# Splitting the first transfers and widening a normalisation in a two-layer hybrid attention kernel

## The chip, the cores and the metric

The kernel runs on one core of one Trainium2 chip. A core has five engines that run side by side, each with its own queue of instructions: TensorE (PE; its weight loads are listed as PEld), VectorE (DVE), ScalarE (ACT), GpSimd (POOL) and SyncE (SP), which here issues all the transfers (DMA) between the chip's main memory and the on-chip memory. The metric is the device time of one execution in microseconds (us); less is better.

## The reference

Two layers, each on 256 positions of 1024 values:

```python
h = x @ w_in                      # split into gm_u, gm_v, gm_z, nq, nkc, ... , mq, mz
y_gm  = gmlp_mixer(gm_u, gm_v, gm_z, ...)      # gated MLP over chunks of 128 positions
y_nsa = nsa_mixer(...)            # compressed, selected and windowed attention, gated
y_mem = memory_mixer(mq, mz, mem, w_mem_kv)    # attention over 256 memory rows
y = concatenate([y_gm, y_nsa, y_mem]) @ w_out
x = layer_norm(ALPHA * x + y, ln_g, ln_b)

# gmlp_mixer
u = gelu(u); v = gelu(v).reshape(B, S, 4, 64)
v = layer_norm(v, ln_g, ln_b)     # mean and variance over the 64 values of each group
s = einsum('gij,bnjgc->bnigc', ws * causal, v) + bs
return u * s * silu(z)
```

## The kernel before, in words

Values are float32. For a product, each operand is split into a high part, which ScalarE casts to the type that TensorE reads (a CAST in the trace), and a low part, which VectorE subtracts (`split`); a product is three matmuls, high by high, high by low and low by high (`mm3`). So every weight chunk of 128 x 512 values costs one transfer of 256 KB, one cast and one subtraction, and then its matmuls. A weight matrix is eight such chunks (`weights`, `eighth`), one for each 128 of the 1024 input values. Tile `w` holds the split chunk, and the raw chunk lies in `wr` or, where that is idle, in another tile (`gz`, `mz`, `gu`, `gv`, `kmr`, `vmr`, `qr`, `nz`), so a transfer into `gz` at the start is the first weight chunk and one into `mz` the second.

At the start `load_T` brings the transposed x in five pieces: two of 128 KB (x pieces 0 and 1, for input values 0 to 127 and 128 to 255) and three of 256 KB (two pieces' worth each). Their raw tile is called `dup`. The weights of tile B (keys) come in between, chunk by chunk. `proj` multiplies 128 positions of x with the chunks of a weight matrix, chunk by chunk into one accumulator of 128 x 512, and `keys` uses it for both halves of the positions with B. Before the first data arrive, nine multiplications of a zeroed tile (`warm`, tile `pr`) are in TensorE's queue.

In `gmlp` the normalisation goes over eight units, two position blocks times four groups, of 128 x 64 values in tile `gv`. Mean and variance come from two small instructions per unit (`gst`, `gmv`), the reciprocal root from one VectorE instruction and a power on GpSimd (`veps`, `grs`), then each unit is normalised by one instruction with two scalars per row, and all are multiplied with the weights and added to the bias in `glt` (tile `qr`) by two wide instructions. TensorE then multiplies with the causal matrix, and VectorE applies bias and gate (`gv<-tp,pt,gu`).

The order of all instructions is not the order of the code. Each call is recorded by the class `Plan`, with its cost from a formula (`cost`, lines 138 to 164) and its dependences (`record`). `schedule` searches 1000 times, with random changes to priorities, for the order with the least modelled length (`pack` places instructions by list scheduling, each engine in order), and `emit` issues that order. A number in `nc.rank` overrides the priority: the first x pieces have rank 2 times their index, B's chunk k has 2k + 1, and a lower rank goes first. At most eight transfers are in flight. As the search records everything through one line, all instructions in the profile carry the line number 336, and the tile names tell them apart.

Of the kernel before, what the change touches and what calls it, by code (L numbers as in the profile page):

```python
# [14 lines left out]
ALU = mybir.AluOpType  # L15
# [3 lines left out]
P = 128  # L19
S = 256  # L20
NB = S // P
# [3 lines left out]
HD = 64  # L25
# [10 lines left out]
SB, SN, S0, ZP = (2,), (0, 1), (0, 1, 2), ()  # L36
ORDER = "FWDMNERGPQ01", "WDFMNERGP0Q1"
WARM, WN = 9, 512
XV, BFIRST = (), 0
WIDE = (20, 20)  # L40
PHASE = (3, 0)

# [48 lines left out]
class Plan:  # L91
# [45 lines left out]
    @staticmethod  # L137
    def cost(engine, op, out, ins, kw):
        n = int(np.prod(out.shape[1:]))
        if engine == "tensor":  # L140
            if op == "transpose":
                return 110.0
            if ins[0].dtype == F32:
                return 2 * (55 + 0.42 * n)
            return max(0.4453 * n + 4, 108.0 if ins[0].dtype == F32R else 30.0)
        if "dma" in op:
            return 500.0
        src = max([int(np.prod(a.shape[1:])) for a in ins] + [1])
        in_psum = any(a.tensor._space == PSUM for a in ins)
        if engine == "scalar":  # L150
            extra = sum(isinstance(kw.get(k), bass.AP) for k in ("bias", "accum_out")) + (op == "mul" and len(ins) > 1)
            return (52 if in_psum else 97) + n / 1.2 + 93 * extra
        if engine == "gpsimd":
            if op == "tensor_scalar":
                return (60 if n < 8 else 240) + 0.87 * n
            if op == "tensor_tensor" and n <= 8:
                return 300 + 165 * n
            return 160 + 2.1 * n
        if op == "reciprocal":
            return 60 + 8.3 * n  # L160
        one = 62 * sum(int(np.prod(a.shape[1:])) == 1 for a in ins)
        if not in_psum and op in ("tensor_copy", "tensor_scalar", "tensor_scalar_add"):
            return 65 + 0.52 * n + one
        return 70 + 1.04 * max(src, n) + one
# [14 lines left out]
    def record(self, eng, op, args, kw):  # L179
        aps = [a for a in list(args) + list(kw.values()) if isinstance(a, bass.AP)]  # L180
        out = [args[0]] + ([kw["accum_out"]] if "accum_out" in kw else [])
        dma = "dma" in op
        o = {"i": len(self.ops), "eng": eng, "op": op, "args": args, "kw": kw, "pre": set(), "dma": dma, "rank": self.rank,
             "table": {AF.Exp: "exp", AF.Tanh: "exp", AF.Gelu: "gelu"}.get(args[2]) if op == "activation" else None,
             "cost": self.cost(eng.name, op, args[0], aps[1:], kw),
             "port": not dma and self.shares(eng.name, op, args[0], aps[1:])}
        if dma:
            o["bytes"] = int(np.prod(args[0].shape)) * 4
            o["issue"] = self.DMA_ISSUE[hasattr(args[1].tensor, "subtile_deps")]
        for ap in aps:  # L190
            name = ap.tensor.name
            if not hasattr(ap.tensor, "subtile_deps"):
                continue
            w = any(ap is x for x in out)
            p0, p1, mask = self.region(ap)
            psum = ap.tensor._space == PSUM
            keep = []
            for e in self.live.setdefault(name, []):
                q0, q1, m, ew, j = e
                if psum:  # L200
                    hit = w or ew or self.ops[j]["eng"] is not eng
                else:
                    hit = (w or ew) and p0 < q1 and q0 < p1 and mask & m
                if j != o["i"] and hit:
                    o["pre"].add(j)
                    if w and p0 <= q0 and q1 <= p1 and (mask & m) == m:
                        continue
                keep.append(e)
            keep.append((p0, p1, mask, w, o["i"]))
            self.live[name] = keep  # L210
        if self.after is not None:
            o["pre"].add(self.after)
        self.ops.append(o)
# [126 lines left out]
def hymba_kernel(ctx: ExitStack, tc: tile.TileContext, xT, xN, memT, w512, wC, cw1, par, gln, lngb, const, out):  # L340
# [30 lines left out]
    def split(h, l, src, eng=None):  # L371
        nc.scalar.copy(h, src)
        (eng or nc.vector).tensor_sub(l, src, h)


    def load_T(src, hl, tag, urgent=False):

        for half in range(2):
            raw = buf(tag, [P, 4, S])
            for k0, k1 in ([(0, 1), (1, 2), (2, 4)], [(0, 2), (2, 4)])[half]:  # L380
                ks = slice(4 * half + k0, 4 * half + k1)
                nc.rank = 2 * ks.start if urgent else None
                nc.sync.dma_start(raw[:, k0:k1], src[:, ks])
                h, l = [t[:, ks] for t in hl]
                if urgent and ks.start in XV:
                    nc.vector.tensor_copy(h, raw[:, k0:k1])
                    nc.vector.tensor_sub(l, raw[:, k0:k1], h)
                else:
                    split(h, l, raw[:, k0:k1])
        nc.rank = None  # L390

    def eighth(name, l, k):

        t = buf("w", [P, 2 * NCC], F32R)
        if name == "W1":
            t = t[:, :8 * P].rearrange("p (j h n) -> p h j n", j=4, h=2)
            src = cw1[l, k].rearrange("p (j n) -> p j n", j=4)
        else:
            n = NCC if name == "C" else 512
            t = t[:, :2 * n].rearrange("p (h n) -> p h n", h=2)  # L400
            src = wC[l, k] if name == "C" else (w512[int(name[1]), W512.index("M"), k] if name[0] == "M" else w512[l, W512.index(name), k])
        early = (name, l) == ("B", 0)
        nc.rank = 2 * k + (1 if k or not BFIRST else -1) if early else None
        raws.append(None)
        tags = IDLE.get((name, l), [])
        i = len(raws) % (len(tags) + 4)
        raw = buf(EARLY[k] if early else tags[i] if i < len(tags) else "wr", [P] + list(src.shape)[1:])
        nc.sync.dma_start(raw, src)
        split(t[:, 0], t[:, 1], raw)
        nc.rank = None  # L410
        return t

# [3 lines left out]
    def mm3(acc, a, b, first, last, **kw):  # L416
# [2 lines left out]
        nc.tensor.matmul(acc, ah, bl, start=False, stop=False, **kw)  # L419
        nc.tensor.matmul(acc, al, bh, start=False, stop=last, **kw)  # L420

    def proj(tT, w, b, c0, n, acc):
        ts = slice(b * P, (b + 1) * P)
        for k in range(KC):
            mm3(acc, [x[:, k, ts] for x in tT], [w[k][:, j, c0:c0 + n] for j in range(2)], k == 0, k == KC - 1)
        return acc

    def projT2(tT, w, c0):
# [119 lines left out]
    for l in range(L):  # L548
# [33 lines left out]
            stack_q(qs[:, :, :, b * P:(b + 1) * P], tp.rearrange("p (x n) -> p x n", x=4), SCALE)  # L582

        wb, wa = weights("B", l), weights("A", l)
        for b in range(NB):
            keys(b, proj(x_T, wb, b, 0, 512, bank("acc")))
            queries(b, proj(x_T, wa, b, 0, 512, bank("acc")))
# [27 lines left out]
        def gmlp(gu, gv, glt):  # L615
            st = buf("gst", [P, NB * G, 6], F32)
            mv = buf("gmv", [P, NB * G, 2], F32)
            units = [(i, gv[:, i // G, i % G * HD:(i % G + 1) * HD]) for i in range(NB * G)]
            for i, v in units:
                nc.vector.bn_stats(st[:, i, :], v)  # L620
                nc.vector.bn_aggr(mv[:, i, :], st[:, i, :])
            rs = buf("grs", [P, NB * G], F32)
            rstd_of(rs, mv[:, :, 1])
            for i, v in units:
                nc.vector.tensor_scalar(v, v, mv[:, i, 0:1], rs[:, i:i + 1], ALU.subtract, ALU.mult)
            nc.vector.tensor_mul(gv, gv, glt[:, 0:1, :].to_broadcast([P, NB, 256]))
            nc.vector.tensor_add(gv, gv, glt[:, 1:2, :].to_broadcast([P, NB, 256]))
            nc.gpsimd.tensor_mul(gu, gu, gz)
            gs = bank("tp").rearrange("p (g b d) -> p g b d", g=G, b=NB)
            for g in range(G):  # L630
                nc.tensor.matmul(gs[:, g], wsT[:, g, :], gv[:, :, g * HD:(g + 1) * HD], start=True, stop=True)
            for g in range(G):
                c = slice(g * HD, (g + 1) * HD)
                nc.vector.scalar_tensor_tensor(gv[:, :, c], gs[:, g], bsT[:, g:g + 1], gu[:, :, c], ALU.add, ALU.mult)
            tp = bank("tp")
            for c in range(2):
                for b in range(NB):
                    nc.tensor.transpose(tp[:, (NB * c + b) * P:(NB * c + b + 1) * P], gv[:, b, c * P:(c + 1) * P], ident)
            t3 = tp.rearrange("p (c t) -> p c t", c=2)
            h, lo = [t[:, :2, :] for t in y_T]  # L640
            nc.scalar.mul(h, t3, 0.5)
            nc.vector.scalar_tensor_tensor(lo, t3, 0.5, h, ALU.mult, ALU.subtract)
# [380 lines left out]
```

## Time and profile before

| | |
|---|---|
| median of 3 runs | 295.34 us (295.31 to 295.97) |
| the profiled execution | 295.48 us |
| its span, first to last instruction | 293.7 us |
| instructions | 5787 |

The profile is of one execution. Its times are counted from the first instruction, and the rest of the execution's time lies around the span. Busy time is the time in which an engine had an instruction under way; the ends of matmuls are modelled. In a row of the timeline stand the start, the time to the end of the row's last instruction, the engine, the operation, the tile written and the tiles read, shapes, the number of instructions, and in brackets how long the engine was idle before and what it waited for. The 40 slices of the page show TensorE at 8 or 9 tenths until the last three.

### The profile page before, as it was taken

The page shows a single profiled execution, that of the slowest core. Times are in us where ns is not written, and L with a number is a line of the kernel's source. Part 1 is how long each engine was busy: PE and PEld are TensorE (multiplying, and loading weights), DVE is VectorE, ACT ScalarE, POOL GpSimd, SP SyncE. Part 2 cuts the span into 40 slices and gives each one's busy share as a digit, 9 for nine tenths or more (in the row PEclk, how much of TensorE's full clock was granted, in tenths as well). Part 3 has the DMA queues.
Part 4 walks back from the last instruction along what each step waited for, and adds up shares of the span by engine and source line. Part 5 has one row for each costly group of instructions (what it writes and reads, how often), then busy time and mean ns, then how long its engine had stood idle before and what let it go on. Part 6 is the DMA issues. An engine that isn't in the chain of part 4 may idle for free.

```text
span 293.7 us, 5787 instructions
## 1 busy us (share of the span) xinstructions
PE 281.6 (96%) x1837; PEld 248.1 (84%) x1837; DVE 266.2 (91%) x662; ACT 224.9 (77%) x537; POOL 64.2 (22%) x89
## 2 busy tenths in 40 slices
PE   8999999999999999999999999999999999899990
PEld 3688899988999899777778888898998899687890
DVE  3889889789979998999999998899899999999985
ACT  4877786888998877999776177689969979989400
POOL 0003029304220435020010100491201146000011
PEclk9999999999999999999999999999999999999996
DMA  6999897597766715677257739847685433300012
GB/s 190 388 389 388 251 264 225 141 265 222 236 159 182 233 39 158 209 232 208 72 161 211 225 97 259 271 136 252 190 233 172 121 134 105 111 36 0 2 71 73
DMA packets 30062, 53.66 MB, mean 183 GB/s; under 512 B 3536, under 2 KB 6352, under 8 KB 29904
## 3 DMA queue, kind: packets, MB, share of 16 engines
q1 hardware_dynamic: 30032, 53.30, 58.6%
q8 instruction: 14, 0.23, 0.3%
q14 instruction: 16, 0.13, 0.2%
HBM read 49.09 MB, written 1.05 MB: 171 GB/s over the span
## 4 chain that ended last, share of the span: by engine, by line
PE 63%; ACT 15%; DVE 12%; DMA 5%; issue 3%; SPq 0%; DVEq 0%; ACTq 0%
PE o L336 31%; PE acc L336 22%; PE tp L336 6%; ACT w L336 5%; PE sc L336 3%; ACT pr L336 3%; DVE w L336 2%; DMA wr<-in_w_dram 2%; DMA dup<-dup 2%; DMA mz<-in_w_dram 1%; ACT dup L336 1%; DVE gv L336 1%; DVE pr L336 1%; ACT pTh L336 1%; ACT csTr L336 1%
## 5 line engine op out<-in xcount | busy, mean ns | idle before, releaser
L336 DVE TENSOR_TENSOR w<-wr,w 128x512 fp32r<-128x512 f32 (+1 forms) x84 | 58.9, 715 | 4.8 <-ACT w L336 4.7
L336 PE MATMUL acc<-w,xTh 128*128 128x512 f32 (+2 forms) x208 | 58.3, 349 | 0.0
L336 ACT CAST w<-wr 128x512 fp32r<-128x512 f32 (+1 forms) x84 | 50.6, 624 | 6.3 <-DMA wr<-in_w_dram 2.2
L336 PE MATMUL o<-xTh,w 128*128 128x256 f32 x224 | 44.6, 284 | 0.1
L336 PE MATMUL acc<-w,yTh 128*128 128x256 f32 (+1 forms) x160 | 44.2, 344 | 0.4 <-ACT yTh L336 0.4
L336 POOL TENSOR_SCALAR pr<-pr,fs 128x256 f32<-128x256 f32 (+1 forms) x36 | 23.9, 674 | 92.6 <-DVE fs L336 52.1
L336 PEld LDWEIGHTS acc<-w,xTh 128*128 128x128 f32 x208 | 36.8, 189 | 5.2 <-ACT w L336 0.3
L336 PEld LDWEIGHTS o<-xTh,w 128*128 128x128 f32 x224 | 35.7, 189 | 0.8 <-DVE yt L336 0.3
L336 PE MATMUL acc<-w,xTl 128*128 128x512 f32 (+2 forms) x104 | 35.7, 349 | 0.0
L336 ACT ACTIVATE pr<-pr,nm 128x128 f32<-128x128 f32 (+1 forms) x64 | 28.7, 451 | 9.0 <-DVE nm L336 8.9
L336 PE MATMUL o<-w,xTh 128*128 128x512 f32 (+2 forms) x112 | 35.1, 374 | 0.4 <-DVE w L336 0.2
L336 PE MATMUL o<-xTl,w 128*128 128x256 f32 x112 | 31.3, 283 | 0.0
L336 PEld LDWEIGHTS acc<-w,yTh 128*128 128x128 f32 x160 | 27.2, 188 | 4.3 <-ACT yTh L336 1.1
L336 POOL TENSOR_TENSOR dup<-pr,pt 64x120 f32<-64x120 f32 x32 | 21.8, 692 | 37.2 <-ACT pr L336 30.6
L336 PE MATMUL acc<-w,yTl 128*128 128x512 f32 (+1 forms) x80 | 27.1, 347 | 0.1
L336 PEld LDWEIGHTS o<-w,xTh 128*128 128x128 f32 x112 | 20.1, 189 | 5.2 <-DVE w L336 1.2
L336 DVE TENSOR_TENSOR pTl<-tp,pTh 128x512 fp32r<-128x512 f32 x32 | 21.4, 678 | 0.6 <-ACT pTh L336 0.4
L336 PE MATMUL tp<-ct,pr 128*128 128x128 f32 x128 | 21.7, 275 | 0.2 <-DVE pr L336 0.2
L336 PEld LDWEIGHTS acc<-w,xTl 128*128 128x128 f32 x104 | 19.5, 188 | 2.3
L336 PEld LDWEIGHTS o<-xTl,w 128*128 128x128 f32 x112 | 20.9, 188 | 0.3
L336 ACT CAST pTh<-tp 128x512 fp32r<-128x512 f32 x32 | 18.4, 586 | 3.0 <-PE tp L336 1.7
L336 PE MATMUL o<-w,xTl 128*128 128x512 f32 (+2 forms) x56 | 20.5, 366 | 0.0
(202 smaller groups left out, 705.2 us busy)
## 6 DMA issues: line engine op xcount, KB each, us to landing
wr<-in_w_dram SPq DMA_DIRECT2D x69, 256.0 KB, 3.4
gz<-in_w_dram SPq DMA_DIRECT2D x14, 256.0 KB, 2.9
mz<-in_w_dram SPq DMA_DIRECT2D x14, 256.0 KB, 3.6
gu<-in_w_dram SPq DMA_DIRECT2D x8, 256.0 KB, 4.0
wr<-in_cw_dram SPq DMA_DIRECT2D x8, 256.0 KB, 3.6
dup<-in_lngb_dram SPq DMA_DIRECT2D x4, 512.0 KB, 5.3
wr<-in_wC_dram SPq DMA_DIRECT2D x7, 268.0 KB, 5.7
gv<-in_w_dram SPq DMA_DIRECT2D x7, 256.0 KB, 3.5
```

Of the source, the lines that this page charges most:

```text
L336: getattr(o["eng"].engine, o["op"])(*o["args"], **o["kw"])
```

## The change

There are three edits. First, x piece 0 comes as two transfers of 128 positions each, and B's first weight chunk as two transfers of 256 columns each, each half with its own cast and subtraction; in `proj` the matmuls of the first chunk of B in layer 0 are done by column halves. Second, in `gmlp` the eight narrow normalising instructions become two wide ones with broadcast operands (subtract the mean, multiply with the reciprocal root), and the weights are multiplied in between. Third, some prices of the search change: ScalarE instructions on fewer than 128 rows cost 60 ns more, GpSimd's general price rises by 40 ns and by 40 more for fewer rows, and the masked maximum (`tensor_tensor_reduce`) loses 62 ns.

```diff
@@ Plan.cost
-            return (52 if in_psum else 97) + n / 1.2 + 93 * extra
+            return (52 if in_psum else 97) + n / 1.2 + 93 * extra + (60 if out.shape[0] < P else 0)
...
-            return 160 + 2.1 * n
+            return 200 + 2.1 * n + (40 if out.shape[0] < P else 0)
...
-        one = 62 * sum(int(np.prod(a.shape[1:])) == 1 for a in ins)
+        one = 62 * sum(int(np.prod(a.shape[1:])) == 1 for a in ins) if op != "tensor_tensor_reduce" else 0
@@ Plan.record
-                    hit = w or ew or self.ops[j]["eng"] is not eng
+                    hit = j != o["i"] and (w or ew or self.ops[j]["eng"] is not eng)
@@ load_T
-                nc.sync.dma_start(raw[:, k0:k1], src[:, ks])
-                h, l = [t[:, ks] for t in hl]
-                if urgent and ks.start in XV:
...
-                    split(h, l, raw[:, k0:k1])
+                for ts in [slice(0, P), slice(P, S)] if urgent and not ks.start else [slice(0, S)]:
+                    nc.sync.dma_start(raw[:, k0:k1, ts], src[:, ks, ts])
+                    split(*[t[:, ks, ts] for t in hl], raw[:, k0:k1, ts])
+                    nc.rank = nc.rank if nc.rank is None else nc.rank + 1.5
@@ eighth
-        nc.sync.dma_start(raw, src)
-        split(t[:, 0], t[:, 1], raw)
+        n = src.shape[-1]
+        for cs in [slice(0, n // 2), slice(n // 2, n)] if early and not k else [slice(0, n)]:
+            nc.sync.dma_start(raw[..., cs], src[..., cs])
+            split(t[:, 0, ..., cs], t[:, 1, ..., cs], raw[..., cs])
@@ proj   (first = wb in layer 0, else None)
-            mm3(acc, [x[:, k, ts] for x in tT], [w[k][:, j, c0:c0 + n] for j in range(2)], k == 0, k == KC - 1)
+            cut = n // 2 if w is first and not k else n
+            for c in range(0, n, cut):
+                mm3(acc[:, c:c + cut], [x[:, k, ts] for x in tT], [w[k][:, j, c0 + c:c0 + c + cut] for j in range(2)],
+                    k == 0 and c == 0, k == KC - 1, **({"skip_group_check": True} if w is first else {}))
@@ gmlp
-            for i, v in units:
-                nc.vector.tensor_scalar(v, v, mv[:, i, 0:1], rs[:, i:i + 1], ALU.subtract, ALU.mult)
+            g3 = gv.rearrange("p b (g d) -> p (b g) d", g=G)
+            nc.vector.tensor_sub(g3, g3, mv[:, :, 0].unsqueeze(2).to_broadcast([P, NB * G, HD]))
             nc.vector.tensor_mul(gv, gv, glt[:, 0:1, :].to_broadcast([P, NB, 256]))
+            nc.vector.tensor_mul(g3, g3, rs.unsqueeze(2).to_broadcast([P, NB * G, HD]))
             nc.vector.tensor_add(gv, gv, glt[:, 1:2, :].to_broadcast([P, NB, 256]))
```

## Rows read from the trace of the kernel before

**Rows 1.** The page's totals: busy us (share of the span), instructions.
```profile
PE 281.6 (96%) x1837; PEld 248.1 (84%) x1837; DVE 266.2 (91%) x662; ACT 224.9 (77%) x537; POOL 64.2 (22%) x89
```
**Rows 2.** Busy time by stretch: start:end, length, each engine, PEclk, DMA share, GB/s.
```profile
30.00:270.00 240.00, 236.93 (x1604) 212.79 (x1603) 224.64 (x586) 198.60 (x490) 58.79 (x79) 1.00 0.59 177
285.00:293.70 8.70, 1.32 (x12) 1.11 (x10) 4.94 (x12) 0.00 (x0) 0.99 (x1) 0.73 0.18 61
...
250.00:255.00 5.00, 4.11 (x23) 2.86 (x24) 4.89 (x15) 4.79 (x13) 0.61 (x1) 1.00 0.37 99
```
**Rows 3.** SP's timeline at the start: the first transfer's issue.
```profile
0.72 0.39 SPq L336 DMA_DIRECT2D dup<-in_xT_dram  x1
```
**Rows 4.** Chain of waits, its first long piece: start, us, what.
```profile
2.10 4.05 DMA mz<-in_w_dram
```
**Rows 5.** ScalarE's timeline at the start.
```profile
3.53 0.41 ACT L336 CAST xTh<-dup 128x256 fp32r<-128x256 f32 x1 [1.53 <-DMA dup<-in_xT_dram]
...
6.18 0.62 ACT L336 CAST w<-mz 128x512 fp32r<-128x512 f32 x1 [1.00 <-DMA mz<-in_w_dram]
7.78 0.62 ACT L336 CAST xTh<-dup 128x512 fp32r<-128x512 f32 x1 [0.98 <-DMA dup<-in_xT_dram]
```
**Rows 6.** TensorE's timeline at the start: warm-ups, the second chunk's work, a weight load.
```profile
3.70 1.49 PE L336 MATMUL o<-pr 128*128 128x512 bf16 x3
6.85 0.50 PE L336 MATMUL o<-w,xTh 128*128 128x512 f32 x1 [0.21 <-ACT w L336]
7.58 0.51 PE L336 MATMUL o<-w,xTh 128*128 128x512 f32 x1 [0.23 <-DVE w L336]
12.01 0.19 PEld L336 LDWEIGHTS o<-w,xTh 128*128 128x128 f32 x1 [0.23 <-DVE w L336]
```
**Rows 7.** Busy time by stretch, the transfers' rate in its last column.
```profile
4.00:7.00 3.00, 2.79 (x9) 1.43 (x7) 1.59 (x4) 1.64 (x3) 0.00 (x0) 1.00 0.84 253
```
**Rows 8.** TensorE's timeline: starts of 512-column and of 256-column matmuls.
```profile
7.92 0.40 PE L336 MATMUL o<-w,xTl 128*128 128x512 f32 x1
8.16 0.39 PE L336 MATMUL acc<-w,xTl 128*128 128x512 f32 x1
...
243.00 0.28 PE L336 MATMUL o<-xTl,w 128*128 128x256 f32 x1
243.12 0.28 PE L336 MATMUL o<-xTh,w 128*128 128x256 f32 x1
```
**Rows 9.** VectorE: narrow and wide instructions (timeline; groups by shape; tile gv).
```profile
236.87 1.20 DVE L336 TENSOR_SCALAR gv<-gv,gmv,grs 128x64 f32<-128x64 f32 x5
229.79 0.67 DVE L336 TENSOR_TENSOR w<-wr,w 128x512 fp32r<-128x512 f32 x1
230.39 1.27 DVE L336 TENSOR_TENSOR pTl<-tp,pTh 128x512 fp32r<-128x512 f32 x2
L336 DVE TENSOR_TENSOR pr<-pr,fs 128x640 f32<-128x640 f32 x4 | 3.3, 816 | 0.0
L336 DVE TENSOR_TENSOR w<-gv,w x10: 637/681/932, 9.8 to 262.2; 128x512 fp32r<-128x512 f32 x9, 128x536 fp32r<-128x536 f32 x1
```
**Rows 10.** Layer 1's gMLP: GpSimd's timeline, chain of waits, ScalarE's timeline.
```profile
233.46 1.66 POOL L336 TENSOR_TENSOR grs<-veps,nhalf 128x8 f32<-128x8 f32 x1 [9.73 <-DVE veps L336]
236.95 1.12 DVE gv L336 x5
240.32 0.48 ACT L336 ACTIVATE pr<-sc,nm 128x256 f32<-128x256 f32 x1 [2.00 <-DVE gv L336]
```
**Rows 11.** VectorE's timeline: an idle time behind layer 0's normalisation.
```profile
114.20 2.00 DVE L336 TENSOR_TENSOR w<-wr,w 128x512 fp32r<-128x512 f32 x3 [0.88 <-ACT w L336]
```
**Rows 12.** Repriced instructions: two starts on VectorE; a group by shape.
```profile
247.29 0.42 DVE L336 CUSTOM_DVE_ANT_0 pr<-sc,ct 128x256 f32<-128x256 f32 x1
247.63 0.42 DVE L336 CUSTOM_DVE_ANT_0 pr<-sc,ct 128x256 f32<-128x256 f32 x1
L336 POOL TENSOR_TENSOR dup<-pr,pt 64x120 f32<-64x120 f32 x32 | 21.8, 692 | 37.2 <-ACT pr L336 30.6 <-DMA pr<-pr 5.5
```

More of the change, by code (lines that the diff above doesn't have):

```diff
@@ L38 @@
 WARM, WN = 9, 512
-XV, BFIRST = (), 0
+BFIRST = 0
 WIDE = (20, 20)
@@ L382, in load_T @@
                 nc.rank = 2 * ks.start if urgent else None
-                nc.sync.dma_start(raw[:, k0:k1], src[:, ks])
-                h, l = [t[:, ks] for t in hl]
-                if urgent and ks.start in XV:
-                    nc.vector.tensor_copy(h, raw[:, k0:k1])
-                    nc.vector.tensor_sub(l, raw[:, k0:k1], h)
-                else:
-                    split(h, l, raw[:, k0:k1])
+                for ts in [slice(0, P), slice(P, S)] if urgent and not ks.start else [slice(0, S)]:
+                    nc.sync.dma_start(raw[:, k0:k1, ts], src[:, ks, ts])
+                    split(*[t[:, ks, ts] for t in hl], raw[:, k0:k1, ts])
+                    nc.rank = nc.rank if nc.rank is None else nc.rank + 1.5
         nc.rank = None
@@ L420, in mm3 @@
         nc.tensor.matmul(acc, al, bh, start=False, stop=last, **kw)
+    first = None
     def proj(tT, w, b, c0, n, acc):
@@ L584, in hymba_kernel @@
         wb, wa = weights("B", l), weights("A", l)
+        first = wb if l == 0 else None
         for b in range(NB):
```

## The prediction

> **What bounds the kernel now.** The page's totals first [rows 1]: TensorE shows work for 281.6 of 293.7 us, VectorE for 266.2, ScalarE for 224.9. The reader is to see that TensorE is nearly never free, so the time is TensorE's work plus its gaps plus the end. The table by stages [rows 2] says where the gaps are: from 30 to 270 us TensorE is busy 236.93 of 240.00 us, so all its gaps there sum to 3.07 us; from 285 us on it is done, and VectorE's last normalisation and the store fill the rest, which the change doesn't touch. So the start and the 3.07 us in the middle can be won or lost, and nothing at the end. The largest single middle gap lies at 250 to 255 us, where TensorE has 4.11 of 5.00 us [rows 2].
>
> At the start, SP's timeline, ScalarE's, TensorE's and the head of the chain of waits are read together. SP sends x piece 0, weight chunk 0, x piece 1 and weight chunk 1, the first at 0.72 [rows 3] and the fourth at 2.10 us [rows 4], so one each 0.46 us. The chain begins with the fourth of them: chunk 1's transfer, 2.10 to 6.15 us, then its cast, its low part on VectorE and the multiplications of chunk 1. ScalarE sits idle 1.00 us until that chunk lands at 6.18, and 0.98 us more until x pieces 2 and 3 land at 7.78 [rows 5]. TensorE works on its warm-up multiplications until 5.19 (3.70 + 1.49), with the first real one queued behind them, and then waits for chunk 1 at 6.85 and 7.58 [rows 6]. What starves TensorE at the start is therefore the second chunk, not the first.
>
> **Edit 1: the first x piece and the first weight chunk in two transfers each.** SP's order goes by rank: x piece 0's left half (0), both chunk halves (1), x's right half (1.5), x piece 1 (2), chunk 1 (3). Two issues more stand ahead of chunk 1 and of all that follows.
> - First multiplication: the halves can land earlier, but it can't start earlier, because the warm-ups are ahead of it in TensorE's queue up to 5.19 us [rows 6]. Gain 0. Without that cover the gain would be at most 0.6 us, from the 0.62 us cast of the whole chunk becoming one of about 0.41 (the 128x256 form) and a landing some 0.4 earlier [rows 5].
> - Chunk 1: issued two slots of 0.46 us later, at 3.03 instead of 2.10. If it still takes 4.05 us it lands 0.93 us later: that is one end. The other end is 0: the bytes ahead of it are the same 512 KB, and at 253 GB/s in 4 to 7 us [rows 7] their queue may hide the later issue. Before the change 1024 KB had been issued by 3.0 us, after it 512 KB, so the stream runs a little empty early; I take the middle, 0.45 us. The chunks behind it are late by the same, and TensorE, whose weight loads still wait for a fresh chunk at 12.01 us [rows 6], has no spare work to cover it. It could be below 0 only if fewer transfers in flight sped up chunk 1 by more than 0.93 us of its 4.05; I see no row for that.
> - Extra casts and subtractions: from the two forms, 0.41 and 0.62 us for 256 and 512 columns, 128 columns take about 0.31. x costs 2 x 0.31 - 0.41 = 0.21, the chunk 2 x 0.41 - 0.62 = 0.20 on ScalarE, and VectorE about as much. Both fit in the 1.00 us for which ScalarE waits ahead of chunk 1 [rows 5]; 0 (without that cover 0.4).
> - Chunk 0's six multiplications of 512 columns become twelve of 256: 512-column ones start 0.235 us apart, 256-column ones 0.12 [rows 8], so 6 x 0.235 = 1.41 against 12 x 0.12 = 1.44. Taken as 0.
>
> Sum of edit 1: +0.45 us (0 to +0.93).
>
> **Edit 2: the gMLP normalisation.** Per layer eight TENSOR_SCALAR of 128x64 go, and two TENSOR_TENSOR of 128x512 come beside the two that stay. Five of the narrow ones in a row take 1.20 us at 0.31 each, so they start (1.20 - 0.31)/4 = 0.22 us apart; a wide one keeps VectorE 0.60 us (229.79 to 230.39) [rows 9]. 8 x 0.22 - 2 x 0.60 = 0.58 us of VectorE less per layer. That the added operands are broadcast should cost nothing: the 128x640 product with a broadcast factor takes 0.82 us for 640 columns, no more per column than the plain ones [rows 9].
>
> The row shows that a narrow instruction is nearly all fixed cost. A rule speaks against the edit: the Trainium skill, "VectorE: DVE Perf Modes", section "The perf-mode tier table", lets fp32 tensor_scalar stream two elements a cycle and tensor_tensor one. By it alone, at that page's 0.96 GHz, the eight would stream for 0.27 us and the two for 1.07, an estimated loss of 0.8 us per layer instead of the gain of 0.58. The durations above include whatever the chip did, so they decide; rival 4 holds the rest.
>
> In layer 1 this lies on the path: the chain of waits runs over VectorE through the normalising instructions up to an exponential that ScalarE starts at 240.32 us after 2.00 us of waiting [rows 10], and goes on over ScalarE to the gap at 250 to 255 us, which is 0.89 us long. Shortened by 0.58, ScalarE's casts and VectorE's gMLP product at 251 us are next late, and they come forward with the chain: -0.58 (ends -0.89 and 0). In layer 0 the same instructions lie scattered among other work, and behind them VectorE still idles 0.88 us for ScalarE at 114.20 [rows 11]: 0. That two of the four wide steps no longer wait for GpSimd's power is worth 0: the power ended at 235.1 (233.46 + 1.66) [rows 10], and the run of five that depend on it came at 236.87 [rows 9].
>
> **Edit 3: other prices, so another order.** All instructions are placed by a search over modelled costs. Changed prices and another list of instructions change its result everywhere, not only at the edits. The masked maximum of 256 columns was priced 398 ns and is now 336; on the chip it comes every 345 ns. GpSimd's 64x120 additions were priced 412, now 492, measured 692 [rows 12]. Both move towards the measurement, and the 64 maxima (by the code, over both layers and shapes) free 64 x 0.062 = 4.0 us of planned VectorE time. What a better order can win is bounded by the 3.07 us of gaps; what a worse one can lose I bound by as much, since the present gaps show what one order leaves. I take -0.4 us, about an eighth of the gaps, because these prices got nearer.
>
> **Sum.** The profiled execution took 295.48 us (293.7 us span and 1.8 around it), 0.14 over the median of 295.34. +0.45 - 0.58 - 0.4 = -0.53; 295.34 - 0.53 = 294.8 us.
>
> **Rivals.**
> 1. The new order closes most gaps. For it: the prices of VectorE, which TensorE waits for, are nearer. Against it: the gaps are already short and spread. Two thirds of 3.07 us, and edit 2, less edit 1: 295.34 - 2.05 - 0.1 = 293.2 us.
> 2. Slower by the later second chunk. Place: SP's queue before chunk 1. Price: two slots, 0.93 us, on all of B's chunks, while edit 2's gain is absorbed by ScalarE and the order is as good as before: 296.3 us. It decides once chunk 1's cast starts at 7.0 us or later. For it: the chain begins with that issue [rows 4], and TensorE is fed from hand to mouth until 12 us. Against it: a gap at 250 us set by VectorE and ScalarE would shrink by part of the delay.
> 3. The new order opens gaps elsewhere, half as much again as there are: 295.34 + 1.5 = 296.8 us. For it: the search draws at random and doesn't know the real queues. Against it: the nearer prices.
> 4. Edit 2 loses, because two streams of broadcast operands take longer than the plain ones. For it: 128x512 instructions on the same tile went up to 0.93 us beside other work [rows 9], and at that price the two take 1.86 us against 8 x 0.22 = 1.78, a loss of 0.1 per layer; edit 1 costs its 0.45: 295.34 + 0.45 + 0.1 = 295.9 us. Against it: most of their kin take 0.68. The rule named above points the same way, and the chance covers it.
>
> **How the numbers follow.** Forecast 0.37, rival 1 0.30, rival 2 0.13, rival 3 0.16, rival 4 0.04. A measurement tells about 0.3% from no change, 0.89 us: faster is below 294.45, slower above 296.23. The forecast's own range, 294.0 to 295.7, puts 0.11 of its 0.37 into faster and 0.26 into same. Rival 1 is faster (0.30); rival 2 is slower but for 0.04; rival 3 slower but for 0.01; rival 4 is same. Faster 0.41, same 0.35, slower 0.24. The range reaches from rival 1's better half, 292.6, to rival 3's price, 297.0.
>
> **What would show it.** The first real multiplication no earlier than the warm-ups' end; chunk 1's issue near 3.0 and its cast at 6.4 to 6.8 instead of 6.18; two wide gMLP instructions per layer of 0.67 to 0.8 us, none of 128x64; TensorE's busy time from 30 to 270 us above 236.93 of 240. It is wrong if chunk 1 lands no later and the start gets shorter, if the gaps between 30 and 270 us grow by over a microsecond, or if the last matmul's distance to the end changes.

## The result: slower by 1.0%, and the profile after

The changed kernel takes 298.95 us (median of 7 runs) against 295.44 us for the one before (7 runs on the same chip): ratio 1.0103, 95% interval 1.0072 to 1.0134, so 2.1 to 4.0 us slower. The forecast was 294.8 us, the range 292.6 to 297.0. The profiled execution took 298.21 us with a span of 296.4, where the one before took 295.48 with 293.7.

The page's totals of the kernel after answer to [rows 1]:

```profile
PE 282.2 (95%) x1843; PEld 248.7 (84%) x1843; DVE 265.6 (90%) x652; ACT 228.4 (77%) x541; POOL 65.0 (22%) x89
```

TensorE works 0.6 us longer, with six more multiplications (chunk 0's, cut in halves); the other 2.1 of the 2.7 us are idle time. The table by stages says where. First the kernel before, in stretches that were not shown (start:end, length, each engine's busy time, the granted clock, the transfers' share, GB/s):

```profile
0.00:13.00 13.00, 11.39 (x36) 6.25 (x37) 6.87 (x12) 8.05 (x13) 0.38 (x6) 1.00 0.80 275
95.00:120.00 25.00, 24.74 (x202) 24.00 (x201) 23.49 (x54) 20.63 (x59) 10.04 (x13) 1.00 0.46 146
120.00:140.00 20.00, 19.54 (x109) 15.29 (x108) 19.77 (x65) 19.31 (x53) 2.83 (x4) 1.00 0.72 218
3.00:5.00 2.00, 2.00 (x7) 0.66 (x6) 0.65 (x2) 1.25 (x3) 0.00 (x0) 1.00 0.94 279
8.00:13.00 5.00, 5.00 (x21) 3.38 (x20) 4.45 (x7) 4.49 (x8) 0.00 (x0) 1.00 1.03 390
```

The same view of the kernel after; its second and third lines answer to [rows 2]:

```profile
0.00:13.00 13.00, 10.43 (x36) 5.98 (x36) 5.48 (x11) 6.66 (x12) 0.38 (x6) 1.00 0.71 234
30.00:270.00 240.00, 235.82 (x1601) 211.80 (x1600) 223.07 (x573) 200.73 (x488) 62.01 (x80) 1.00 0.59 179
250.00:255.00 5.00, 4.52 (x37) 4.14 (x37) 4.94 (x19) 4.77 (x14) 1.20 (x1) 1.00 0.23 55
95.00:120.00 25.00, 24.44 (x199) 23.64 (x198) 21.79 (x52) 20.08 (x54) 8.21 (x13) 1.00 0.45 137
120.00:140.00 20.00, 18.54 (x106) 14.42 (x106) 19.62 (x60) 19.84 (x52) 2.57 (x3) 1.00 0.77 237
3.00:5.00 2.00, 2.00 (x7) 0.81 (x6) 1.14 (x3) 0.81 (x3) 0.00 (x0) 1.00 0.63 165
8.00:13.00 5.00, 3.60 (x13) 2.00 (x12) 2.66 (x4) 2.95 (x5) 0.00 (x0) 1.00 0.95 333
```

Two places lose. Up to 13 us TensorE idles 2.57 us instead of 1.61 (+0.96). From 30 to 270 us it idles 4.18 instead of 3.07 (+1.11), and one stage, 120 to 140 us, gives nearly as much by itself: 18.54 busy instead of 19.54. The other stages' losses and gains cancel (95 to 120 us loses 0.30). The gap at 250 to 255 us, which edit 2 aimed at, did get shorter there.

The start, SP's timeline of the kernel after (start, us, queue, instruction), beside [rows 3, 4]:

```profile
0.72 0.39 SPq L336 DMA_DIRECT2D dup<-in_xT_dram  x1
1.17 0.90 SPq L336 DMA_DIRECT2D gz<-in_w_dram  x2
2.11 0.91 SPq L336 DMA_DIRECT2D dup<-in_xT_dram  x2
3.05 0.43 SPq L336 DMA_DIRECT2D mz<-in_w_dram  x1
...
4.95 0.43 SPq L336 DMA_DIRECT2D dup<-in_xT_dram  x1
```

Chunk 1 (mz) is issued at 3.05, as forecast, and x pieces 4 and 5 at 4.95 instead of 4.00. ScalarE's timeline after (in brackets the idle time before and what ended it), beside [rows 5]:

```profile
3.43 0.89 ACT L336 CAST w<-gz 128x256 fp32r<-128x256 f32 x2 [0.42 <-DMA gz<-in_w_dram]
...
6.39 0.62 ACT L336 CAST w<-mz 128x512 fp32r<-128x512 f32 x1 [0.22 <-DMA mz<-in_w_dram]
8.06 0.62 ACT L336 CAST xTh<-dup 128x512 fp32r<-128x512 f32 x1 [1.05 <-DMA dup<-in_xT_dram]
...
11.72 0.62 ACT L336 CAST xTh<-dup 128x512 fp32r<-128x512 f32 x1 [1.47 <-DMA dup<-in_xT_dram]
```

Chunk 1 is cast at 6.39, 0.21 us late. The larger delay is behind it: x pieces 4 and 5 are cast at 11.72, and before the change that was this row of ScalarE's timeline; the second row is from e3, an experiment told below, whose first transfers are those of the kernel before:

```profile
9.86 0.62 ACT L336 CAST xTh<-dup 128x512 fp32r<-128x512 f32 x1
10.40 0.62 ACT L387 CAST xTh<-dup 128x512 fp32r<-128x512 f32 x1
```

So the cast is 1.86 us late in this pair of traces, but one trace against one can't size it. In the twelve traces whose first transfers go as before (the kernel before, e3 to e8, e13 to e15, e17, e18) it comes at 9.68 to 11.15 us, at 10.16 on the mean. In the four with two issues more (after, e1, e2, e9) it comes at 11.25 to 11.97, at 11.70 on the mean. For the cast of chunk 1 the means are 6.27 and 6.71. So chunk 1 is some 0.4 us late, x pieces 4 and 5 some 1.5. TensorE's timeline after shows what the delays become, and its largest waits of the stage at 120 to 140 us:

```profile
9.65 0.50 PE L336 MATMUL o<-w,xTh 128*128 128x512 f32 x1 [0.67 <-ACT w L336]
...
13.20 0.50 PE L336 MATMUL o<-w,xTh 128*128 128x512 f32 x1 [0.93 <-ACT w L336]
...
126.97 0.38 PE L336 MATMUL sc<-ksh,qs 128*128 128x256 f32 x1 [0.84 <-DVE nm L336]
128.92 0.45 PE L336 MATMUL o<-pTl,vn 128*64 128x512 f32 x1 [0.22 <-DVE pTl L336]
133.74 0.50 PE L336 MATMUL acc<-w,yTh 128*128 128x512 f32 x1 [0.38 <-DVE w L336]
```

### The profile page after: what moved, and what is told of

Read it like the earlier page. It is cut to its first block, busy times and chain, and to the rows that moved or that the text cites. A ratio compares the mean times of both kernels' runs of the same rounds, so it can differ in the third digit from the quotient of the medians.

```text
span 296.4 us, 5803 instructions
## 1 busy us (share of the span) xinstructions
PE 282.2 (95%) x1843; PEld 248.7 (84%) x1843; DVE 265.6 (90%) x652; ACT 228.4 (77%) x541; POOL 65.0 (22%) x89
## 4 chain that ended last, share of the span: by engine, by line
PE 65%; DVE 14%; ACT 9%; DMA 6%; issue 3%; SPq 1%; DVEq 0%; ACTq 0%
PE o L336 30%; PE acc L336 25%; PE tp L336 8%; DVE pr L336 4%; PE sc L336 3%; DVE w L336 3%; DMA kmr<-in_w_dram 2%; ACT w L336 2%; ACT pr L336 2%; DMA wr<-in_w_dram 2%; DMA dup<-dup 2%; SPq L336 1%; DVE pTl L336 1%; ACT pTh L336 1%; DVE xn L336 1%
## 5 line engine op out<-in xcount | busy, mean ns | idle before, releaser
L336 PE MATMUL acc<-w,xTh 128*128 128x512 f32 (+2 forms) x210 | 59.3, 349 | 0.0
L336 PEld LDWEIGHTS acc<-w,xTh 128*128 128x128 f32 x210 | 37.4, 191 | 4.9 <-DVE w L336 0.4
L336 PE MATMUL o<-w,xTh 128*128 128x512 f32 (+2 forms) x114 | 36.7, 374 | 1.6 <-ACT w L336 1.6
L336 POOL TENSOR_TENSOR dup<-pr,pt 64x120 f32<-64x120 f32 x32 | 23.1, 735 | 35.6 <-ACT pr L336 27.8
L336 PE MATMUL acc<-w,yTl 128*128 128x256 f32 (+1 forms) x80 | 27.3, 347 | 0.2 <-DVE yTl L336 0.2
L336 PEld LDWEIGHTS o<-w,xTh 128*128 128x128 f32 x114 | 20.9, 190 | 5.9 <-ACT w L336 2.5
L336 DVE CUSTOM_DVE_ANT_0 pr<-sc,ct 128x128 f32<-128x128 f32 (+1 forms) x64 | 20.3, 349 | 2.1 <-PE sc L336 1.9
```

What stands on the lines that cost most here:

```text
L336: getattr(o["eng"].engine, o["op"])(*o["args"], **o["kw"])
```

## The experiments

To try one edit without a new draw of the search, the order that the search found for the kernel before (or after) was written into the kernel as a list of places, one for each instruction; an added instruction takes the place beside the one that it was cut from (`...` marks where the packed list is read):

```diff
-        for o in self.schedule():
...
+        for o, t in zip(self.ops, place):
+            o["t"] = max([float(t)] + [self.ops[j]["t"] + 1e-3 for j in o["pre"]])
+        for o in sorted(self.ops, key=lambda o: (o["t"], o["i"])):
```

All times, each with its ratio to runs of the kernel before on the same chip (their medians lay between 294.37 and 295.42 us; the ratio is taken over the single runs and isn't the quotient of two medians; "drawn" is an order from the search, "kept" one from the list):

| run | what differs from before | order | median us | ratio, 95% interval |
|---|---|---|---|---|
| e1 | both code edits | kept, of before | 296.82 | 1.0027 [0.9999, 1.0056] |
| e2 | split only | kept, of before | 296.46 | 1.0027 [0.9999, 1.0054] |
| e3 | wide gMLP only | kept, of before | 295.64 | 0.9998 [0.9972, 1.0025] |
| e4 | wide gMLP, whole transfers | kept, of after | 297.33 | 1.0057 [1.0028, 1.0085] |
| e5 | new prices | drawn, seed 3 | 298.63 | 1.0136 [1.0109, 1.0162] |
| e6 | seed 4 | drawn | 304.62 | 1.0322 [1.0287, 1.0357] |
| e7 | seed 5 | drawn | 302.44 | 1.0247 [1.0207, 1.0287] |
| e8 | new prices, seed 4 | drawn | 298.56 | 1.0139 [1.0112, 1.0166] |
| e9 | two 4 KB transfers on SP | kept, of before | 295.99 | 1.0027 [1.0005, 1.0050] |
| e10 | weight chunk split | kept, of before | 296.10 | 1.0033 [1.0009, 1.0057] |
| e11 | x piece split | kept, of before | 296.12 | 1.0049 [1.0024, 1.0073] |
| e12 | chunks 0, 1 from ScalarE | kept, of before | 294.77 | 0.9994 [0.9971, 1.0018] |
| e13 | as e4, two instructions moved | kept, of after | 298.02 | 1.0097 [1.0073, 1.0122] |
| e14 | seed 6 | drawn | 301.64 | 1.0242 [1.0214, 1.0270] |
| e15 | new prices, seed 5 | drawn | 298.51 | 1.0113 [1.0087, 1.0139] |
| e16 | chunk 0 from ScalarE | kept, of before | 294.22 | 0.9986 [0.9968, 1.0003] |
| e17 | as e4, two VectorE steps left out | kept, of after | 297.27 | 1.0055 [1.0032, 1.0077] |
| e18 | as e17, their casts left out too | kept, of after | 296.40 | 1.0029 [1.0004, 1.0054] |

### Which part of the change costs

**e1_all_old_order**: the diff without its prices, in the order of before.

> All code edits, but the instructions stand in the order of the kernel before (the order written into the file, not searched). Theory start (the two extra issues ahead of the second chunk cost about 2 us at the start, and the redrawn order little): about 297.5 us, the start as in the changed kernel, TensorE's second chunk and the x pieces 4 and 5 late. Theory order (the redrawn order is the loss): 295 us or less, near the kernel before. If both share it: 296.5 to 297.

**e2_split_old_order**: the same without the wide normalisation.

> Only the split of the first x piece and the first weight chunk, narrow normalisation, order of the kernel before. Theory start: 296.8 to 298 us, slower than before by 1.5 to 2.5. Theory order: within 0.5 us of before (the forecast's 0.45 for this edit).

**e3_wide_old_order**: only the wide normalisation.

> Only the wide normalisation, whole first transfers, order of the kernel before. The forecast's step: 0.3 to 0.6 us faster than before (294.9). If wide forms with broadcast operands are dearer: the same or up to 0.5 us slower. Neither theory of the loss expects more than 0.5 us either way.

**e4_whole_new_order**: the order of after, the halves joined again:

```diff
-                for ts in [slice(0, P), slice(P, S)] if urgent and not ks.start else [slice(0, S)]:
+                for ts in [slice(0, P), slice(P, S)] if False else [slice(0, S)]:
...
-        for cs in [slice(0, n // 2), slice(n // 2, n)] if early and not k else [slice(0, n)]:
+        for cs in [slice(0, n // 2), slice(n // 2, n)] if False else [slice(0, n)]:
...
-            cut = n // 2 if w is first and not k else n
+            cut = n
```

> The changed kernel in its own order, written into the file, but with the first x piece and the first chunk as whole transfers again. Theory start: it gets back to 296 to 297 us, some 2 us under the changed kernel's 298.95. Theory order: it stays at 298 to 299. If both share it: about 297.5.

The split costs about 0.8 us (0.27%, with an interval from 0 to 0.54%), the wide normalisation nothing that can be told, the order 1.7 us (0.57%). The two parts that cost add to 2.5 us, inside the 2.1 to 4.0 of the whole: both share the loss, as e1 and e4 were to show by their middle ranges, while e2 lies between its two theories. The stage from 120 to 140 us shows the order's part by itself: TensorE's busy time there is 19.54 to 19.58 us in e1, e2 and e3, and in e4, line for line as in after:

```profile
120.00:140.00 20.00, 18.54 (x99) 13.63 (x98) 19.68 (x61) 19.82 (x54) 2.71 (x3) 1.00 0.72 226
```

Why the wide normalisation wins nothing is in e3's table by stages and ScalarE's timeline:

```profile
228.00:250.00 22.00, 21.92 (x181) 21.32 (x179) 20.77 (x58) 19.83 (x50) 10.03 (x11) 1.00 0.40 121
250.00:255.00 5.00, 4.09 (x23) 2.89 (x24) 4.89 (x15) 4.90 (x13) 0.61 (x1) 1.00 0.37 104
```
```profile
235.69 0.48 ACT L387 ACTIVATE pr<-sc,nm 128x256 f32<-128x256 f32 x1
240.43 0.48 ACT L387 ACTIVATE pr<-sc,nm 128x256 f32<-128x256 f32 x1 [2.00 <-PE tp L387]
```

The kernel before, the first of these rows:

```profile
235.58 0.47 ACT L336 ACTIVATE pr<-sc,nm 128x256 f32<-128x256 f32 x1
```

VectorE is 0.46 us freer at 228 to 250 us (20.77; the kernel before has 21.23). But ScalarE's exponential, which stood at 240.32 behind VectorE [rows 10], still starts at 240.43 after the same 2.00 us, now released by TensorE, which has 21.92 of 22.00 us there with either normalisation. The two timelines stand 0.11 us apart ahead of the last normalising steps (235.58 and 235.69) and 0.11 behind them (240.32 and 240.43), so in this stage the edit won nothing. The gap at 250 us stays as it was (4.09, before 4.11 [rows 2]). The time of e3 alone wouldn't settle it: the forecast's 0.58 us is 0.2%, and the interval reaches 0.28% below 1.

### The start: what delays the stream

**e9_two_small**: nothing split; two transfers of 4 KB behind chunk 0.

```diff
+    few = buf("few", [P, 16], F32)
+    for i in range(2):
+        nc.record(nc.sync, "dma_start", (few[:, 8 * i:8 * i + 8], const[:, 8 * i:8 * i + 8]), {}, at=13)   # behind chunk 0
```

> The kernel before (its order, whole transfers) with two extra transfers of 4 KB each issued from SP right behind weight chunk 0, so everything after is issued two slots (about 0.93 us) later, and two more transfers are in flight; no extra casts and the 512 KB of the first pieces go as before. Theory issue slots (the loss at the start of the split is the two SP issues): x pieces 4 and 5 are cast at 11.3 to 11.9 us instead of 9.86, time 296.3 to 297. Theory small transfers (the loss is that halves of 128 KB move slower than pieces of 256 KB): x pieces 4 and 5 within 0.5 us of before, time 295.2 to 295.9.

Theory issue slots, by the start; the time came out 0.3 us under its range. SP's timeline of e9 shows the two extra issues, ScalarE's has x pieces 4 and 5 as late as the real split (e1: 11.85, e2: 11.25), with nothing else changed, and its table by stages has the same weak stream:

```profile
1.64 0.90 SPq L391 DMA_DIRECT2D few<-in_const_dram  x2
```
```profile
11.97 0.62 ACT L391 CAST xTh<-dup 128x512 fp32r<-128x512 f32 x1 [1.46 <-DMA dup<-in_xT_dram]
```
```profile
3.00:5.00 2.00, 2.00 (x6) 0.47 (x4) 0.43 (x1) 0.78 (x2) 0.00 (x0) 1.00 0.67 176
8.00:13.00 5.00, 4.24 (x15) 2.58 (x15) 2.59 (x5) 2.85 (x5) 0.00 (x0) 1.00 0.97 349
```

The last column is what to read: 176 GB/s at 3 to 5 us, after 165, before 279 (208 to 307 in the twelve traces with the first transfers of before). By 3.0 us SP had issued 1024 KB before the change; after it and in e9 512 KB. So two issues more are enough for the late start. Whether it is SP's time or the added transfers themselves isn't separated: those of e9 are small but come in 128 rows of 32 bytes each.

**e10_split_chunk** and **e11_split_x**: one of the two split, so one slot more.

> The kernel before (its order) with only the first weight chunk in two transfers. One more SP issue ahead of chunk 1. Both theories of the start: half of the loss of the whole split, 295.7 to 296.1 us, x pieces 4 and 5 cast at 10.4 to 11.0 us. If the halves of the chunk are what costs and those of x do not: 296.2 to 296.7 us here.

> The kernel before (its order, but for the first two matmuls, of which that on the left half of x comes first) with only the first x piece in two transfers. Issue slots: as for the chunk, 295.7 to 296.1 us, x pieces 4 and 5 cast at 10.4 to 11.0 us. If x halves are what costs (512-byte rows instead of 1 KB): 296.2 to 296.7 us here and nothing in the run that splits only the chunk.

Both have the cast where the theories put it (10.47 and 10.48), but that lies inside the 9.68 to 11.15 us of the traces without any extra issue, so no delay is shown by it. The stream at 3 to 5 us is as weak as with two slots (172 and 176 GB/s), though 768 KB had been issued by 3.0 us: the bytes issued by then don't set it. Where ScalarE's third table load stands (ACT_TABLE_LOAD, the same place in the kept order) tells how late the work is by then. The kernel before, e9 and e10:

```profile
76.37 1.28 ACT L336 ACT_TABLE_LOAD   x1
77.70 1.28 ACT L391 ACT_TABLE_LOAD   x1
76.20 1.28 ACT L387 ACT_TABLE_LOAD   x1
```

With two slots it is 0.7 to 1.3 us late (e1 77.50, e2 77.09), with one slot on time (e11 76.40). The times say otherwise: one slot was to cost half, and the ratios of e10 and e11 are no smaller than those of e2 and e9, from which they can't be told apart. So two slots cost, and what one slot costs stays open.

**e12_two_queues** and **e16_chunk0_other_queue**: the opposite of the change, SP relieved.

```diff
-            nc.sync.dma_start(raw[..., cs], src[..., cs])
+            (nc.scalar if early and k < 2 else nc.sync).dma_start(raw[..., cs], src[..., cs])   # e16: k < 1
```

> The kernel before (its order, whole transfers) with weight chunks 0 and 1 of B issued from ScalarE instead of SP, so SP's later issues come two slots (about 0.93 us) earlier: the opposite of what the change did. Theory issue slots: x pieces 4 and 5 are cast about 0.9 us earlier (near 9.0), chunk 1 about 0.5 us earlier, time 294.3 to 294.9 us, faster than both kernels. Theory small transfers or bandwidth (the bytes set when things land, not the issues): casts within 0.3 us of before, time 295.1 to 295.9 us.

> The kernel before (its order, whole transfers) with only weight chunk 0 of B issued from ScalarE, so that SP's later issues come one slot (0.47 us) earlier and chunk 1 doesn't compete with the first x piece. Theory issue slots: x pieces 4 and 5 cast at 9.2 to 9.6 us, first x cast at 3.5 to 3.7 (with both chunks moved: 4.36), time 294.4 to 295.0, ratio 0.996 to 0.999. Theory bytes (the stream is at the rate of its transfers once eight are in flight): casts as before, ratio 0.999 to 1.001.

The casts of x pieces 4 and 5 came near where the slots put them, at 9.24 and 9.20 (9.68 at the earliest without), and the stream moved 385 and 369 GB/s from 5 to 8 us (before 279). The Trainium skill, "Trainium Kernel Development and Optimization", section "Key Constraints", says that issuing from several engines at once saves only the issue time, as all share the same DMA engines. The trace of e12 agrees: 0.9 us earlier than the mean of 10.16, for two slots of 0.47. Two other expectations missed: chunk 1 was not cast 0.5 us earlier in e12 (6.54), and the first x piece, expected at 3.5 to 3.7 in e16, is cast at 5.05 (4.36 in e12) instead of 3.53 [rows 5]. The first transfers now share the stream, and in e16 TensorE runs out of warm-ups:

```profile
2.43 2.28 PE L387 MATMUL o<-pr 128*128 128x512 bf16 x6
6.03 0.51 PE L387 MATMUL o<-w,xTh 128*128 128x512 f32 x1 [1.33 <-ACT w L387]
```

Both spans are 291.9 us, 1.8 below the profiled one of before, but those are among the fastest executions of their twelve, and over 12 runs each neither ratio is clear of 1. A version better than both kernels is pointed to here and not shown.

### The order: worse prices, or a good draw lost

**e5_prices_only**: the kernel before with the three new prices and nothing else. **e6_seed4**, **e7_seed5**, **e14_seed6**: the kernel before with another seed. **e8_prices_seed4**, **e15_prices_seed5**: both.

```diff
-    ROUNDS, TRIES, SEED = 8, 1000, 3
+    ROUNDS, TRIES, SEED = 8, 1000, 4
```

> The kernel before with only the three new prices of the planner, so the search draws another order; whole first transfers, narrow normalisation. Theory prices (the new prices lead the search into slower orders): 296.5 to 298 us, ratio 1.004 to 1.008, and TensorE's busy time in 120 to 140 us below 19.0 of 20 as in the order of after (18.54). Theory draw (any new list of instructions or prices is a new draw, and draws scatter by 1 to 2 us either way): anything from 294 to 297.5 us, with its gaps at other places than 120 to 140 us.

> The kernel before with another seed of the planner's search, old prices, nothing else. Theory prices: an old-price order is good, so 295.0 to 295.9 us, within 0.2% of before. Theory draw: the order of before was a good draw, so 295.5 to 297.5 us, slower than before by 0.1 to 0.7%.

> As the run with seed 4, with seed 5. Theory prices: 295.0 to 295.9 us. Theory draw: 295.5 to 297.5 us, and not the same as seed 4 (over 0.5 us apart).

> New prices and seed 4. Theory prices: slower than seed 4 with the old prices by 1 to 2 us, as the new-price order of after was against that of before. Theory draw: it stands to seed 4 with old prices in no fixed way; within 2 us on either side of 296.5 us.

> The kernel before with seed 6 and the old prices. Two fresh draws with old prices took 302.4 and 304.6 us, three orders drawn with new prices 297.3 to 298.6. Theory good draw (the order of before is the lucky one of its kind): 300 to 305 us. Theory two kinds of seeds (old prices as good as new ones on average): 295 to 299.

> The kernel before with the new prices and seed 5. Theory that the new prices make the usual draw better, and only the kept draw of the old ones is better still: 297 to 299.5 us. Theory that prices don't matter and draws scatter by 10 us: anything from 295 to 305.

Of the first four, none came inside a range that had been written down for it: the draws scatter more than either theory allowed. The theory that the new prices lead to worse orders falls: at seeds 4 and 5 they give the better one (1.0139 after 1.0322, 1.0113 after 1.0247). Three other seeds with the old prices give 1.0242 to 1.0322, three with the new ones 1.0113 to 1.0139, on the mean 1.0270 and 1.0129; by three draws each this is 1.4%, and half of it with seed 3 counted among the old ones. The order of before was no ordinary draw: it is the best of the four with old prices, by 2.4% or more.

The prices alone cost more (e5, 4.0 us) than the order of after does in e4, at the same seed. The change's new list of instructions draws again, too; no run draws that list with the old prices, so how the 1.7 us divide between prices and list isn't shown.

### What is wrong in the new order at 120 to 140 us

**e13_two_moved**: e4 with two places of the list changed, so that VectorE serves the awaited masked maxima (nm) 0.94 us of work earlier (written here as what it does; the kernel holds the reordered list):

```diff
+PLACE[1410] = PLACE[1402] + 0.3   # another masked maximum
+PLACE[1529] = PLACE[1408] + 0.3   # low part of weight chunk 11
```

> The order of after with whole first transfers (as the run e4_whole_new_order: 297.33 us), with two of VectorE's instructions moved behind the two masked maxima for which TensorE waits 0.84 us in the stage from 120 to 140 us: the low part of one weight chunk (0.60 us, not needed until some 3 us later) and one other masked maximum (0.34 us). TensorE's order and all else stay. Theory local order (what stands ahead of the awaited instruction makes the gap): the 0.84 us wait falls below 0.1, TensorE's busy time at 120 to 140 us rises from 18.54 to about 19.3, time 296.4 to 296.8 us. Theory full engine (VectorE is busy 19.6 of 20 us there, so the gap only moves on): another wait of 0.5 us or more for VectorE appears behind it, busy time at 120 to 140 us stays at 18.5 to 18.8, time 297.1 to 297.5.

TensorE's waits in e4 are those of after (0.84, 0.22, 0.38). In e13:

```profile
124.93 0.39 PE L387 MATMUL sc<-ksh,qs 128*128 128x256 f32 x1 [0.33 <-DVE nm L387]
127.83 0.44 PE L387 MATMUL o<-pTl,vn 128*64 128x512 f32 x1 [0.68 <-DVE pTl L387]
132.64 0.50 PE L387 MATMUL acc<-w,yTh 128*128 128x512 f32 x1 [0.38 <-DVE w L387]
```

The gap only moved on (0.51 us less in one row, 0.46 more in the next), as it would behind a full engine; TensorE's busy time there is 18.36, and the time was no better.

**e17_two_left_out**: e4 with 1.2 us of VectorE's work gone: the low parts of two weight chunks aren't computed.

```diff
-        for o in sorted(self.ops, key=lambda o: (o["t"], o["i"])):
+        for o in sorted([o for o in self.ops if o["i"] not in (1526, 1529)], key=lambda o: (o["t"], o["i"])):   # e18: also 1525, 1528, their casts
```

> As e4_whole_new_order (order of after, whole first transfers; 297.33 us, ratio 1.0057), but two of VectorE's 0.60 us instructions of the stage from 120 to 140 us are left out: the low parts of two weight chunks of layer 1, whose multiplications use stale values, so this part of the result isn't computed. Theory full engine: TensorE's waits for VectorE in this stage (0.84, 0.38 and 0.22 us in e4) go almost altogether, its busy time there rises from 18.54 to 19.4 or more, time 296.0 to 296.5, ratio 1.001 to 1.004. Theory of the one awaited instruction in e13's sense, or of something else than VectorE's load: the busy time stays under 19.0 and the time within 0.4 us of e4.

**e18_two_chunks_left_out**: the same chunks' casts on ScalarE gone too.

> As e17_two_left_out, and the two ScalarE casts (0.52 us apart each) of the same two weight chunks of layer 1 are left out too, so the splitting of these two chunks isn't computed. Theory both engines full (VectorE 19.68, ScalarE 19.82 of 20 us in e4): TensorE's gaps from 120 to 140 us shrink from 1.5 to under 0.8 us, time 296.0 to 296.6. Theory spread order (each of the gaps has a chain of its own, and removing a microsecond of work on both engines only shifts them): busy time at 120 to 140 us stays under 18.9, time 297.0 to 297.6.

The stage in e17 and in e18:

```profile
120.00:140.00 20.00, 18.47 (x102) 13.92 (x101) 19.23 (x61) 19.82 (x54) 2.25 (x3) 1.00 0.70 242
```
```profile
120.00:140.00 20.00, 19.16 (x109) 14.56 (x107) 19.59 (x61) 19.57 (x54) 2.29 (x4) 1.00 0.75 244
```

Relieving VectorE alone changes nothing; ScalarE (fourth busy time, 19.82 of 20) is just as full, which fits, and one of TensorE's waits in the stage is now for ScalarE (0.29 us), but the others are still for VectorE (0.47, 0.39, 0.38). Relieving both gives TensorE 0.62 of its lost 1.0 us back, to 0.84 us of gaps where under 0.8 was expected. The time follows in the right direction (1.0057 to 1.0029), but the intervals overlap.

What fills the two engines is seen by asking for the weight tiles alone (tile w on ScalarE: start:end, length, busy time). The kernel before, then after:

```profile
70.00:120.00 50.00, 16.14 (x27) 1.00 0.57 175
120.00:140.00 20.00, 4.91 (x8) 1.00 0.72 218
```
```profile
70.00:120.00 50.00, 10.73 (x19) 1.00 0.47 147
120.00:140.00 20.00, 8.38 (x14) 1.00 0.77 237
```

The order of before casts 27 chunks ahead of the stage and 8 in it; the new one 19 and 14, and the low parts on VectorE move likewise (18.92 to 13.72 us ahead of the stage). So did the six orders drawn in the experiments: ScalarE has 10.6 to 14.0 us of these casts at 70 to 120 us, and TensorE 17.1 to 18.4 busy of 20 us behind them (in e5 at a granted clock of 0.91). But late casts are not the whole of it: e8 has 5.40 us of them in the stage, hardly more than before, and ScalarE busy for only 18.00, yet TensorE has 18.41, and its large wait there is 1.24 us for another cast (pTh).

Part of ScalarE's lateness can be seen in its table loads, the groups of before and after:

```profile
L336 ACT ACT_TABLE_LOAD x5 | 6.4, 1283 | 0.8 <-PEq L1012 0.7
L336 ACT ACT_TABLE_LOAD x7 | 9.0, 1283 | 0.8 <-PEq L1020 0.7
```

The new order changes between the exponential and GELU once more to and fro; the two further loads of 1.28 us (four stand at 68 to 84 us instead of two) take 2.6 of the 3.5 us by which ScalarE's total grew. No run tests what they cost, and they aren't what makes a draw slow in general: seeds 5 and 6 with the old prices have five loads, too, and take some 302 us.

The other stages can't be sized so: from 180 to 215 us the same order gives TensorE 33.38 us in e4 and 34.66 in after (before 34.15), a scatter from run to run, while 120 to 140 us has 18.54 in both.

## Why the prediction was wrong

**Edit 1**, forecast +0.45 us with ends 0 and +0.93, measured about +0.8 (0 to 1.6). The direction was right, and e9 shows that two more issues do it without any split; that the cost goes by the slot isn't borne out (e10, e11). Wrong was the step "the chunks behind it are late by the same". Chunk 1 itself is about as late as forecast (0.21 us in the pair of traces, 0.44 on the means); its 4.05 us in flight [rows 4] became 3.3. The stream behind it, weak at 3 to 5 us, hands x pieces 4 and 5 over later still, 1.5 us on the means. The number was taken from the transfer that the chain of waits named, and the larger delay fell on a later one. The halves did come early (first chunk half cast at 3.43) and won nothing behind the warm-ups, as forecast.

**Edit 2**, forecast -0.58, measured 0 by the timelines, which stand as far apart behind the normalisation as ahead of it (by the time 0.9998, an interval that the forecast would still fit). The instruction costs were right: the wide ones take 0.68 us and VectorE is 0.46 us freer. Wrong was "Shortened by 0.58, ScalarE's casts and VectorE's gMLP product at 251 us are next late, and they come forward with the chain". In that stage TensorE has no gap to give (21.92 of 22 us), and its own product releases the same exponential at the same moment.

**Edit 3**, forecast -0.4, measured +1.7 (0.8 to 2.5), and by far the largest error. The step that failed is the gain taken "because these prices got nearer". It compares a new draw with an ordinary one: the other draws with the new prices were better than those with the old by 1.4%, but the order of before was not an ordinary draw, and with the prices alone the same seed gave an order slower by 4.0 us (e5). The bound of 3.07 us on either side was too narrow as well: e6's gaps from 30 to 270 us are 9.57 us.

Rival 3 (the new order opens gaps, 296.8 us) was the true case, with edit 1's cost on top, and its 1.5 us were near the 1.7 measured; it had 0.16. Of the signs named for being wrong, one came: the gaps from 30 to 270 us grew by 1.11 us, over a microsecond.

**Open:** what one slot costs, and why x pieces 4 and 5 are later than chunk 1; how the order's loss divides between prices and list; what the other 0.4 us of the stage, the two further table loads and the smaller differences of the new order cost; whether a second queue at the start helps.

## What to carry to other kernels

Where instructions are placed by a seeded search, any change of prices or of the list of instructions is a new draw, and its spread (here 7 to 10 us between the order of before and three other seeds) is a term of the sum; run a few seeds of the unchanged kernel before crediting or blaming an edit. A busy chain of waits is worth shortening only where the engine that bounds the stage has a gap to close. At the start of a kernel look beyond the first late transfer: two small ones more delayed those far behind them most. And a time in one trace is sized only when the same time in other traces is known.

## What the runs showed of the hardware that was not expected

Two transfers of 4 KB on one queue, which together took SP 0.90 us to issue (one of 256 KB takes 0.43), were enough to make a 256 KB transfer that is issued 3 us later be cast at 11.97 us, where twelve traces without them have 9.68 to 11.15. With one transfer more on the queue (e10, e11) the work isn't later at 76 us in the trace. With that queue relieved by one issue (e16), the stream ran at 369 GB/s at 5 to 8 us instead of 279, but the first 128 KB were cast 1.5 us later, beside the second queue's transfer.
